# Attention units regrouped: both heads of a pair over 128 queries, scores as three 64-row products per head

## The chip, the cores and the metric

The kernel runs on one core of a Trainium2 chip. The metric is the device time of one execution in microseconds (us); the median of the runs is compared. Durations of single instructions come from one profiled execution.

## What is computed

One decoder layer on x of 1024 positions by 1024 features, float32. After an RMS norm one projection feeds two attention branches of eight heads each (head width 64): branch A is causal attention over the 256 keys that an indexer selects for each query, branch B is a causal dilated attention whose three patterns are merged. Both have an RMS norm on each head's queries and keys and a bias by relative position. Gates, an output projection and the residual follow.

```python
def reference(x, norm_gain, w_in, w_out, rel_bias, q_norm_a, k_norm_a, q_norm_b, k_norm_b):
    ...
        xn = rms_norm(x, norm_gain[layer])
        proj = jnp.einsum('bsd,de->bse', xn, w_in[layer])
        qa, ka, va, za, qi, ki, wi, qb, kb, vb, zb = jnp.split(proj, split_points, axis=-1)
        qa = rms_norm(qa.reshape(b, s, N_HEADS_A, HEAD_DIM), q_norm_a[layer])
        ka = rms_norm(ka.reshape(b, s, N_HEADS_A, HEAD_DIM), k_norm_a[layer])
        ...
        a_out = dsa_attention(qa, ka, va, qi, ki, wi, bias_a)
        b_out = dilated_attention(qb, kb, vb, bias_b)
        mixed = jnp.concatenate([a_out.reshape(b, s, D_A) * jax.nn.silu(za),
                                 b_out.reshape(b, s, D_B) * jax.nn.silu(zb)], axis=-1)
        x = x + jnp.einsum('bse,ed->bsd', mixed, w_out[layer])
    return x
```

In both branches a head's core is softmax(q k^T / 8 + bias + mask) v; the kernel computes it densely over all causal keys, with the selection or the dilation in the bias.

## The kernel before

Every float32 operand of a large product is split into a high part of type fp32r and a remainder ("hi" and "lo"), and a product is taken as two or three products of such parts. The work is done in eight pairs of heads (`make_pair`, L422), each pair's q, k, v and gate columns projected together. For each pair and each of eight blocks of 128 positions, `proj_item` (L434) issues 24 products of 512 columns (L445 to L447), scales and normalises the result, and keeps v as a hi and a lo part (L464 to L466). Its `finish2` (L480) splits k into `k`, where a head's 64 hi columns stand beside its 64 lo columns; `later` (L494) transposes that on TensorE, so that the tile `kst` holds, for each head, 64 rows of hi over 64 rows of lo.

Attention works on units (`make_unit`, L550). A unit is one head of a pair over two query blocks, 2s and 2s+1, that is 256 queries; a pair has four values of s and two heads, eight units in all, 64 in the program.

- `split_q` (L527) writes q as hi, lo, hi in 192 columns per block and head; `transpose_q` (L535) makes of it two stationary operands of 128 rows, hi over lo and lo over hi. For each of the two query blocks it issues four transposes into a PSUM tile (pool tag "tr", one buffer) and ScalarE casts it to `qt` (L544).
- `scores` (L555) takes a query block against up to 512 keys (a chunk): two products of 128 rows (L566, L567), both into one PSUM tile `sp` (tag "s", two buffers). VectorE adds the bias and keeps a running minimum (L573); in branch A, GpSimd first adds the selection mask to the bias (L571). When the last chunk is done, ScalarE takes the exponential and its sum (L583). The results stand in tiles `L` (six buffers, shared with scratch of the key selection).
- `pt` (L594) transposes the exponentials of two key blocks and both query blocks into one PSUM tile of up to 512 columns (L600), and splits it into `pth` (ScalarE, L604) and `ptl` (VectorE, L605).
- `pv` (L608) multiplies by v: for each key block a product of 256 columns (both query blocks) with `pth` and one with `ptl` (L618); the last key block of a unit has 128 columns (L616). The stationary operand is v of one key block and head, 128 columns: hi and lo beside each other.
- `make_gate` and `combine` (L629, L637) add the halves, divide, gate and store.

`run_slot` (L789) sets the order in which all this is written: in slot k stand the scores of unit k+1, the transposes and value products of unit k, the combine of the unit before, a share of the projection of a later pair (`place`, L781, by the table `gw`), and in the first half of the program steps of the key selection on VectorE (L266). The framework's scheduler then orders the instructions of each engine. TensorE takes its queue in order.

Of the kernel before, what the change touches and what calls it, by code (L numbers as in the profile page):

```python
# [10 lines left out]
F32 = mybir.dt.float32  # L11
# [35 lines left out]
def kernel(ctx: ExitStack, tc: tile.TileContext, xT, x, w_idx, w_pair, w_out, gain,  # L47
# [10 lines left out]
    def f32(ap):  # L58
        return ap.bitcast(F32)
# [99 lines left out]
    def dup_hi(t, h):  # L159

        return t.rearrange("p h (a d) -> p h a d", d=HD)[:, :h, 0:3:2, :]
# [272 lines left out]
    def proj_item(p, tb):  # L434
# [45 lines left out]
        def finish2():  # L480
            if j == 1:
                return
            raw, mu = duo["raw"], duo["mu"]
            kk = raw[:, :, 2:4, :]
            p.eng.tensor_tensor(kk, kk, mu[:, :, 2:4].unsqueeze(3).to_broadcast([P, 2, 2, HD]), OP.mult)
            k = rg.tile([P, 2, 2, P], F32R, name="k", tag="ktok", bufs=CFG["kb"])
            nc.scalar.copy(k[:, :, :, 0:64], kk)
            p.eng.tensor_tensor(k[:, :, :, 64:128], kk, f32(k[:, :, :, 0:64]), OP.subtract)
            duo["k"] = k
            q = rg.tile([P, 2, 2, HD], F32, name="q", tag="q", bufs=CFG["q"])  # L490
            p.eng.tensor_tensor(q, raw[:, :, 0:2, :], mu[:, :, 0:2].unsqueeze(3).to_broadcast([P, 2, 2, HD]), OP.mult)
            p.q[tb // 2] = q

        def later():  # L494
            if j == 1:
                return
            pk = ps.tile([P, 2, 2, P], F32R, name="pk", tag="tr", bufs=CFG["tr"])
            for b in range(2):
                for h in range(2):
                    nc.tensor.transpose(pk[:, h, b, :], duo["k"][:, b, h, :], identr)  # L500
# [3 lines left out]
            nc.scalar.copy(p.k[s][:, :, o:o + 2 * P], f32(pk.rearrange("p h b t -> p h (b t)")))  # L504

        it.groups = [lambda kt=kt: group(kt) for kt in range(KT)]
        def weight(kt):
# [18 lines left out]

    def split_q(p, s):  # L527

        q = p.q[s].rearrange("p b h d -> p (b h) d")
        hl = sb.tile([P, 4, 192], F32R, name="qhl", tag="qhl", bufs=CFG["qhl"])  # L530
        nc.scalar.copy(dup_hi(hl, 4), q.unsqueeze(2).to_broadcast([P, 4, 2, HD]))
        p.eng.tensor_tensor(hl[:, :, 64:128], q, f32(hl[:, :, 0:64]), OP.subtract)
        p.hl[2 * s] = p.hl[2 * s + 1] = hl

    def transpose_q(p, s):  # L535
        hl = p.hl[2 * s]
        for qb in (2 * s + 1, 2 * s):
            pq = ps.tile([P, 512], F32R, name="pq", tag="tr", bufs=CFG["tr"])
            for h in range(2):
# [3 lines left out]
            qt = sb.tile([P, 2, 2, P], F32R, name="qt", tag="qT", bufs=CFG["qT"])  # L543
            nc.scalar.copy(qt.rearrange("p a b c -> p (a b c)"), f32(pq))  # L544
            p.hl[qb] = qt

    class Block:
        pass

    def make_unit(p, s, h, blk):  # L550
        u = Unit()
        u.p, u.s, u.h, u.blk = p, s, h, blk
        L, mns = {}, {}

        def scores(qb, ci, last):  # L555
            nk = (qb + 1) * P
            col0 = S - P - P * qb
            c0 = 512 * ci
            w = min(512, nk - c0)
            if qb not in mns:  # L560
                mns[qb] = [sm.tile([P, 2], F32, name="mn", tag="mn"), 0]
            mn, done = mns[qb]
# [5 lines left out]
            l = sb.tile([P, 512], F32, name="L", tag="L", bufs=CFG["L"])  # L568
            bias = p.T[h][:, col0 + c0:col0 + c0 + w]
            if p.is_a and qb >= 2:  # L570
                nc.gpsimd.tensor_tensor(l[:, :w], bias, sc[qb][:, c0:c0 + w], OP.add)  # L571
                bias = l[:, :w]
            nc.vector.tensor_tensor_reduce(l[:, :w], sp[:, :w], bias, -1.0,  # L573
                                           3e38 if done == 0 else mn[:, done - 1:done],
                                           OP.add, OP.min, mn[:, done:done + 1])
            mns[qb][1] = done + 1
            L[qb, ci] = l
            if last:
                j = qb - 2 * s
                for c in range(len(chunks_of(qb))):  # L580
                    w = min(512, nk - 512 * c)
                    l = L[qb, c][:, :w]
                    nc.scalar.activation(l, l, AF.Exp, bias=mn[:, done:done + 1], scale=-1.0,  # L583
                                         accum_out=blk.den[:, j, h, c:c + 1])

        u.S = []
        for qb in (2 * s + 1, 2 * s):
            cs = list(range(len(chunks_of(qb))))[::-1]
            for c in cs:
                u.S.append(lambda qb=qb, c=c, last=(c == cs[-1]): scores(qb, c, last))  # L590

        T = {}

        def pt(kp):  # L594
            t = ps.tile([P, 512], F32, name="pt", tag="ptp", bufs=CFG["ptp"])
            slots = [(2 * kp, 2 * s), (2 * kp, 2 * s + 1)]
            slots += [(2 * kp + 1, 2 * s), (2 * kp + 1, 2 * s + 1)] if kp < s else [(2 * kp + 1, 2 * s + 1)]
            for si, (kb, qb) in enumerate(slots):
                o = (kb % 4) * P
                mark(nc.tensor.transpose(t[:, si * P:(si + 1) * P], L[qb, kb // 4][:, o:o + P], identf))  # L600
            w = len(slots) * P
# [4 lines left out]
            T[kp] = th, tl  # L606

        def pv(kp):  # L608
            if kp == 0 and h == 0:
                blk.po = ps.tile([P, 2, 256], F32, name="po", tag="o", bufs=CFG["o"])  # L610
            po = blk.po
            for j in range(2):
                vv = p.v[kp][:, j, 2 * h:2 * h + 2, :].rearrange("p a b -> p (a b)")
                for n, t in enumerate(T[kp]):
                    if j and kp == s:
                        nc.tensor.matmul(po[:, h, 128:256], vv, t[:, 256:384], start=False, stop=(n == 1))  # L616
                    else:
# [4 lines left out]
        for kp in range(s + 1):  # L622
            u.B.append(lambda kp=kp: pt(kp))
            if kp:
                u.B.append(lambda kp=kp: pv(kp - 1))
        u.B.append(lambda: pv(s))
        return u

    def make_gate(p, s, blk):  # L629
# [90 lines left out]
    for p in pairs:  # L720
        for s in range(3, -1, -1):
            blk = Block()
            blk.p, blk.s = p, s
            for h in range(2):
                units.append(make_unit(p, s, h, blk))

    def unit(k):
        return units[k] if 0 <= k < len(units) else None
# [60 lines left out]
    def run_slot(k):  # L789
# [7 lines left out]
            ev.append(((t - g0) / (g1 - g0), f))  # L797
        att = []
        u = unit(k - 1)
        if u and u.h == 1:  # L800
            att.append(lambda: combine(u.p, u.s, u.blk))
        w = unit(k + 2)
        if w and w.h == 0:
            for h in range(2):
                if h not in w.p.T:
                    ev.append((0.0, lambda h=h: w.p.T.__setitem__(h, load_T(2 * w.p.n + h))))
            ev.append((CFG["sq"], lambda: split_q(w.p, w.s)))
            ev.append((CFG["qt"], lambda: transpose_q(w.p, w.s)))
        a = []
        un = unit(k + 1)  # L810
        if un:
            if un.h == 0:
# [4 lines left out]
        if v and v.h == 1:  # L817
# [82 lines left out]
```

## Time and profile before

| | |
|---|---|
| time, median of 3 runs (lowest to highest) | 821.43 us (818.26 to 826.37) |
| the profiled execution: its own time, and its span | 824.92 us, 823.2 us |
| TensorE (PE) busy, of the span | 774.1 us, 94% |
| TensorE weight loads (PEld) | 658.5 us, 80% |
| VectorE (DVE) | 590.5 us, 72% |
| ScalarE (ACT) | 492.5 us, 60% |
| GpSimd (POOL) | 435.0 us, 53% |
| mean granted clock of TensorE, share of full | 0.975 |

Each TensorE product has a weight load (PEld) and a matmul (PE). Matmuls are pipelined: a record of 0.39 us overlaps the next one's, so the price of a product in a stream is the distance from its start to the next start, not its own duration. A form such as "128*128 128x512" reads: 128 rows by 128 columns of stationary operand, 512 columns streamed, 128 rows of result.

### The profile page before, as it was taken

What the parts mean: (1) busy time and instruction counts of PE and PEld (TensorE: products, weight loads), DVE (VectorE), ACT (ScalarE), POOL (GpSimd) and SP (SyncE); (2) the same over time, 40 slices, a digit from 0 to 9 for tenths busy, and PEclk for the clock granted to TensorE, in tenths of its full rate; (3) what the DMA queues carried; (4) which work ended last, traced back from release to release, by engine and by line L of the source; (5) the groups of instructions that cost most, each with busy time, mean ns of one, the idle gap of its engine ahead of it and who ended that gap; (6) DMA issues with size and microseconds to landing.
All of it is one profiled execution on the core that took longest, in us unless ns stands there. A gap on an engine that the chain in (4) does not pass through costs nothing.

```text
span 823.2 us, 12893 instructions
## 1 busy us (share of the span) xinstructions
PE 774.1 (94%) x4302; PEld 658.5 (80%) x4302; DVE 590.5 (72%) x1366; ACT 492.5 (60%) x1156; POOL 435.0 (53%) x453
## 2 busy tenths in 40 slices
PE   5999989999999999999999699999998998999996
PEld 4778857888888888878887588878887886788874
DVE  6834778878999989997578777567755775667621
ACT  6834466567676766767675376757774675456400
POOL 6942536347533833574278867755555575435320
PEclk9999998999999999999999799999998999999999
DMA  8679005003200510141013100410162225725775
GB/s 296 234 226 297 4 2 189 15 14 103 77 14 14 141 52 1 33 123 53 2 52 103 39 14 14 120 61 14 27 166 77 65 75 184 241 95 193 219 219 183
DMA packets 52053, 83.34 MB, mean 101 GB/s; under 512 B 5632, under 2 KB 23312, under 8 KB 51984
## 3 DMA queue, kind: packets, MB, share of 16 engines
q1 hardware_dynamic: 47376, 74.10, 29.2%
q0 software_dynamic: 4608, 8.39, 3.8%
q8 instruction: 34, 0.56, 0.3%
q14 instruction: 35, 0.29, 0.1%
HBM read 65.62 MB, written 26.29 MB: 112 GB/s over the span
## 4 chain that ended last, share of the span: by engine, by line
PE 35%; DVE 8%; DMA 5%; ACT 2%; issue 1%; POOL 1%; SPq 0%; DVEq 0%; POOLq 0%; ACTq 0%
PE pp L445 4%; PE pp L446 4%; PE pp L447 4%; PE po L618 4%; PE pt L600 4%; PE pp L672 3%; PE pp L674 3%; PE pp L673 3%; PE sp L566 2%; PE sp L567 2%; DVE jk L245 1%; DMA mo<-mixl_d 1%; DVE ptl L605 1%; DMA raw<-in_w_pair_dram 1%; DMA raw<-in_w_out_dram 1%
## 5 line engine op out<-in xcount | busy, mean ns | idle before, releaser
L445 PE MATMUL pp<-wh,xh 128*128 128x512 f32 x512 | 210.7, 414 | 1.0 <-ACT wh L84 1.0
L446 PE MATMUL pp<-wl,xh 128*128 128x512 f32 x512 | 203.2, 397 | 1.4 <-POOL wl L85 1.4
L447 PE MATMUL pp<-wh,xl 128*128 128x512 f32 x512 | 202.9, 397 | 0.0
L583 ACT ACTIVATE L<-L,mn 128x512 f32<-128x512 f32 (+1 forms) x192 | 117.4, 613 | 60.0 <-DVE mn L573 59.2
L571 POOL TENSOR_TENSOR L<-T,sc 128x512 f32<-128x512 f32 (+3 forms) x80 | 90.2, 1150 | 62.1 <-PE pt L600 46.9
L605 DVE TENSOR_TENSOR ptl<-pt,pth 128x512 fp32r<-128x512 f32 (+1 forms) x160 | 100.2, 632 | 30.9 <-ACT pth L604 29.7
L85 POOL TENSOR_TENSOR wl<-raw,wh 128x512 fp32r<-128x512 f32 x68 | 90.9, 1346 | 57.5 <-ACT wh L84 53.1
L604 ACT CAST pth<-pt 128x512 fp32r<-128x512 f32 (+1 forms) x160 | 85.6, 542 | 47.8 <-PE pt L600 45.1
L447 PEld LDWEIGHTS pp<-wh,xl 128*128 128x128 f32 x512 | 97.3, 190 | 19.8
L446 PEld LDWEIGHTS pp<-wl,xh 128*128 128x128 f32 x512 | 98.0, 191 | 17.7 <-POOL wl L85 2.3
L445 PEld LDWEIGHTS pp<-wh,xh 128*128 128x128 f32 x512 | 97.8, 191 | 17.6 <-ACT wh L84 2.2
L600 PE MATMUL pt<-identr,L 128*128 128x128 f32 x576 | 88.1, 275 | 0.8 <-ACT L L583 0.8
L266 DVE TENSOR_SCALAR_CACHE_REDUCE waste<-sc,thr 128x640 int8<-128x640 f32 (+5 forms) x90 | 84.6, 940 | 0.8
L618 PE MATMUL po<-ptl,v 128*128 128x256 f32 x256 | 71.2, 295 | 11.2 <-DVE ptl L605 11.2
L618 PE MATMUL po<-pth,v 128*128 128x256 f32 x256 | 72.8, 295 | 1.6 <-DVE mx L646 1.4
L566 PE MATMUL sp<-kst,qt 128*128 128x512 f32 (+1 forms) x192 | 71.6, 375 | 0.0
L600 PEld LDWEIGHTS pt<-identr,L 128*128 128x128 f32 x576 | 66.2, 141 | 4.7 <-ACT L L583 1.2
L567 PE MATMUL sp<-kst,qt 128*128 128x512 f32 (+1 forms) x192 | 68.2, 355 | 0.0
L84 ACT CAST wh<-raw 128x512 fp32r<-128x512 f32 x80 | 48.5, 618 | 32.7 <-DMA raw<-in_w_pair_dram 24.3
L618 PEld LDWEIGHTS po<-ptl,v 128*128 128x128 f32 x256 | 48.8, 191 | 18.1 <-DVE ptl L605 14.2
L462 POOL TENSOR_TENSOR mu<-ss,mhalf 128x8 f32<-128x8 f32 x32 | 54.4, 1699 | 12.4 <-DVE ss L460 11.5
L453 ACT ACTIVATE praw<-pp,rr 128x512 f32<-128x512 f32 x64 | 43.7, 685 | 28.2 <-PE pp L447 27.8
(150 smaller groups left out, 1677.8 us busy)
## 6 DMA issues: line engine op xcount, KB each, us to landing
raw<-in_w_pair_dram SPq DMA_DIRECT2D x64, 256.0 KB, 2.8
skew<-rowd SPq DMA_DIRECT2D x16, 576.0 KB, 13.9
T<-skew SPq DMA_DIRECT2D x16, 512.0 KB, 3.6
stage<-in_x_dram SPq DMA_DIRECT2D x16, 256.0 KB, 5.4
mixh_d<-mh SPq DMA_DIRECT2D x32, 128.0 KB, 2.2
mixl_d<-ml SPq DMA_DIRECT2D x32, 128.0 KB, 2.1
raw<-in_w_out_dram SPq DMA_DIRECT2D x16, 256.0 KB, 3.3
mo<-mixh_d POOLq DMA_DIRECT2D x16, 256.0 KB, 3.6
```

The costliest lines, as they stand in the source:

```text
L85: (eng or nc.gpsimd).tensor_tensor(lo, raw, f32(hi), OP.subtract)
L445: pace(nc.tensor.matmul(pp, xh[tb][:, kt, :], hi, start=(kt == 0), stop=False))
L446: nc.tensor.matmul(pp, xh[tb][:, kt, :], lo, start=False, stop=False)
L447: nc.tensor.matmul(pp, xl[tb][:, kt, :], hi, start=False, stop=(kt == KT - 1))
L566: mark(nc.tensor.matmul(sp[:, :w], qt[:, h, 0, :], kk, start=True, stop=False))
L567: nc.tensor.matmul(sp[:, :w], qt[:, h, 1, :], kk, start=False, stop=True)
L571: nc.gpsimd.tensor_tensor(l[:, :w], bias, sc[qb][:, c0:c0 + w], OP.add)
L583: nc.scalar.activation(l, l, AF.Exp, bias=mn[:, done:done + 1], scale=-1.0, accum_out=blk.den[:, j, h, c:c + 1])
L600: mark(nc.tensor.transpose(t[:, si * P:(si + 1) * P], L[qb, kb // 4][:, o:o + P], identf))
L604: nc.scalar.copy(th[:, :w], t[:, :w])
L605: nc.vector.tensor_tensor(tl[:, :w], t[:, :w], f32(th[:, :w]), OP.subtract)
L618: nc.tensor.matmul(po[:, h, :], vv, t[:, 256 * j:256 * j + 256], start=(kp == 0 and j == 0 and n == 0), stop=False)
```

## The change

A unit is now one query block of 128 queries for both heads of a pair (still eight units a pair). `k` and `q` are split with the two heads beside each other: one half of the tile holds the hi part of both heads, the other the lo part, so that after the transposes head 0 stands on partitions 0 to 63 and head 1 on 64 to 127. `split_q` no longer writes hi twice, and `transpose_q` issues four transposes and one cast for both query blocks together. A score is three products of 64 rows for each head (hi by hi, hi by lo, lo by hi), written with the heads in turns, each head into its own `sp`. `pt` takes one head and one chunk; `pv` multiplies 128 columns at a time, key block by key block, first all of `pth`, then all of `ptl`. The pool sizes and the table `gw` stay.

```diff
@@ finish2
-            nc.scalar.copy(k[:, :, :, 0:64], kk)
-            p.eng.tensor_tensor(k[:, :, :, 64:128], kk, f32(k[:, :, :, 0:64]), OP.subtract)
+            kk = kk.rearrange("p b h d -> p b (h d)")
+            nc.scalar.copy(k[:, :, 0, :], kk)
+            p.eng.tensor_tensor(k[:, :, 1, :], kk, f32(k[:, :, 0, :]), OP.subtract)
...
@@ split_q, transpose_q
-        nc.scalar.copy(dup_hi(hl, 4), q.unsqueeze(2).to_broadcast([P, 4, 2, HD]))
-        p.eng.tensor_tensor(hl[:, :, 64:128], q, f32(hl[:, :, 0:64]), OP.subtract)
+        nc.scalar.copy(hl[:, :, 0, :], q)
+        p.eng.tensor_tensor(hl[:, :, 1, :], q, f32(hl[:, :, 0, :]), OP.subtract)
...
-        for qb in (2 * s + 1, 2 * s):
-            pq = ps.tile([P, 512], F32R, name="pq", tag="tr", bufs=CFG["tr"])
-            for h in range(2):
-                t = hl[:, 2 * (qb % 2) + h, :]
-                nc.tensor.transpose(pq[:, (2 * h) * P:(2 * h + 1) * P], t[:, 0:128], identr)
-                nc.tensor.transpose(pq[:, (2 * h + 1) * P:(2 * h + 2) * P], t[:, 64:192], identr)
...
+        pq = ps.tile([P, 512], F32R, name="pq", tag="tr", bufs=CFG["tr"])
+        for j in (1, 0):
+            for a in range(2):
+                nc.tensor.transpose(pq[:, (2 * j + a) * P:(2 * j + a + 1) * P], hl[:, j, a, :], identr)
...
@@ scores
-            sp = ps.tile([P, 512], F32, name="sp", tag="s", bufs=CFG["s"])
-            qt = p.hl[qb]
-            kk = p.k[ci][:, h, :w]
-            mark(nc.tensor.matmul(sp[:, :w], qt[:, h, 0, :], kk, start=True, stop=False))
-            nc.tensor.matmul(sp[:, :w], qt[:, h, 1, :], kk, start=False, stop=True)
+            qt, kk = p.hl[u.s], p.k[ci]
+            sp = [ps.tile([P, 512], F32, name="sp", tag="s", bufs=CFG["s"]) for h in range(2)]
+            for n, (a, b) in enumerate(((0, 0), (0, 1), (1, 0))):
+                for h in range(2):
+                    r = slice(HD * h, HD * h + HD)
+                    m = nc.tensor.matmul(sp[h][:, :w], qt[r, j, a, :], kk[r, b, :w], start=(n == 0), stop=(n == 2))
...
@@ pt, pv
-                        nc.tensor.matmul(po[:, h, :], vv, t[:, 256 * j:256 * j + 256],
-                                         start=(kp == 0 and j == 0 and n == 0), stop=False)
...
+            po = blk.po[:, h, P * j:P * j + P]
+            w = min(512, nk - c)
+            for n, t in enumerate(T[h, c]):
+                for o in range(0, w, P):
+                    kb = (c + o) // P
+                    vv = p.v[kb // 2][:, kb % 2, 2 * h:2 * h + 2, :].rearrange("p a b -> p (a b)")
+                    nc.tensor.matmul(po, vv, t[:, o:o + P], start=(c == chunks[0] and n == 0 and o == 0),
+                                     stop=(c == chunks[-1] and n == 1 and o == w - P))
```

How the instructions stand in TensorE's queue is shown at two places. The first is the score products of the first pair where its attention begins; `sp` is the PSUM tile of a score, `kst` the transposed keys, `qt` the transposed queries, `pp` a projection's PSUM tile. Before, a chunk has two products into one tile:

```order
L566 MATMUL sp_1491<-kst_1106,qt_1477 128x512
L567 MATMUL sp_1491<-kst_1106,qt_1477 128x512
L566 MATMUL sp_1507<-kst_1385,qt_1477 128x512
L567 MATMUL sp_1507<-kst_1385,qt_1477 128x512
L445 MATMUL pp_1403<-wh_1305,xh7_464 128x512
L445 MATMUL pp_1460<-wh_1305,xh6_425 128x512
L566 MATMUL sp_1541<-kst_1106,qt_1484 128x384
L567 MATMUL sp_1541<-kst_1106,qt_1484 128x384
```

Now the queue's first scores are these (a "x3" marks three equal rows in a row):

```order
L569 MATMUL sp_1486<-kst_1106,qt_1477 128x512
L569 MATMUL sp_1487<-kst_1106,qt_1477 128x512
L569 MATMUL sp_1486<-kst_1106,qt_1477 128x512
L569 MATMUL sp_1487<-kst_1106,qt_1477 128x512
L569 MATMUL sp_1486<-kst_1106,qt_1477 128x512
L569 MATMUL sp_1487<-kst_1106,qt_1477 128x512
L542 MATMUL pq_1693<-identr_84,qhl_1623 128x128 x4
L445 MATMUL pp_1403<-wh_1305,xh7_464 128x512
L445 MATMUL pp_1460<-wh_1305,xh6_425 128x512
L569 MATMUL sp_1537<-kst_1385,qt_1477 128x512 x3
L446 MATMUL pp_1403<-wl_1306,xh7_464 128x512
L447 MATMUL pp_1403<-wh_1305,xl7_465 128x512
```

The first chunk stands with the heads in turns, as the code writes it; of the second chunk, the three products of head 0 (`sp_1537`) stand together, and those of head 1 follow ten rows of projection later. Over the whole program the 576 score products stand in 165 runs between other work: 27 of them are six products strictly in turns, 60 are three products of a single head, 14 are three of one head followed by three of the other.

The second place is the first value products (`po`) of the same pair, on TensorE too; `pt` is a PSUM tile of transposed exponentials, `v` the values. Before:

```order
L618 MATMUL po_1606<-pth_1579,v_1395 128x256
L618 MATMUL po_1606<-ptl_1580,v_1395 128x256
L600 MATMUL pt_1626<-identr_84,L_1544 128x128
L600 MATMUL pt_1626<-identr_84,L_1494 128x128
L600 MATMUL pt_1626<-identr_84,L_1544 128x128
L600 MATMUL pt_1626<-identr_84,L_1494 128x128
L618 MATMUL po_1606<-pth_1597,v_1264 128x256
L618 MATMUL po_1606<-ptl_1598,v_1264 128x256
L618 MATMUL po_1606<-pth_1597,v_1264 128x256
L618 MATMUL po_1606<-ptl_1598,v_1264 128x256
```

Now:

```order
L615 MATMUL po_1611<-ptl_1577,v_1116 128x128 x2
L615 MATMUL po_1611<-ptl_1577,v_830 128x128 x2
L599 MATMUL pt_1628<-identr_84,L_1498 128x128 x4
L615 MATMUL po_1611<-pth_1588,v_1395 128x128 x2
L615 MATMUL po_1611<-pth_1588,v_1264 128x128 x2
L615 MATMUL po_1611<-ptl_1589,v_1395 128x128 x2
L615 MATMUL po_1611<-ptl_1589,v_1264 128x128 x2
L599 MATMUL pt_1651<-identr_84,L_1547 128x128 x4
```

A value product of 256 columns has become two of 128, each with a weight load of its own; the transposes between them are as many as before. TensorE's queue holds 1152 value products of 128 columns, where it held 512 of 256 and 128 of 128.

## Rows read from the trace of the kernel before

**Rows 1.** By stretch: us; PE, PEld, DVE, ACT, POOL busy; clock; DMA; GB/s

```profile
200.00:300.00 100.00, 98.30 (x581) 84.84 (x580) 90.48 (x253) 68.89 (x165) 55.16 (x65) 1.00 0.24 69
...
sum 823.00, PE 774.08 PEld 658.50 DVE 590.53 ACT 492.51 POOL 434.97; mean PE 77.41 PEld 65.85 DVE 59.05 ACT 49.25 POOL 43.50
```

**Rows 2.** Waits of TensorE: waiter, releaser, us in total, times, longest us

```profile
PE po L618 <- DVE ptl L605: 11.2, 10, 2.3
PE pq L541 <- ACT qt L544: 8.4, 10, 3.6
...
PE pi L176 <- ACT wih L104: 0.3, 1, 0.3
```

**Rows 3.** Groups of TensorE by form: count, busy us, mean ns, idle us before

```profile
L618 PE MATMUL po<-pth,v 128*128 128x256 f32 x256 | 72.8, 295 | 1.6 <-DVE mx L646 1.4
...
L541 PE MATMUL pq<-identr,qhl 128*128 128x128 f32 x128 | 26.6, 254 | 12.2 <-ACT qt L544 8.4 <-POOL qhl L532 2.1 <-ACT kst L504 1.8
...
L616 PE MATMUL po<-pth,v 128*128 128x128 f32 x64 | 14.4, 224 | 0.0
```

**Rows 4.** The score products of line 566: count, durations ns min/median/max, first and last start, forms

```profile
L566 PE MATMUL sp<-kst,qt x192: 220/389/755, 126.4 to 776.9; 128*128 128x512 f32 x96, 128*128 128x384 f32 x32, 128*128 128x256 f32 x32, 128*128 128x128 f32 x32
```

**Rows 5.** TensorE in order of time: start us, duration us, instruction (transposes, value products, scores)

```profile
308.40 0.34 PE L567 MATMUL sp<-kst,qt 128*128 128x384 f32 x1
308.58 0.23 PE L541 MATMUL pq<-identr,qhl 128*128 128x128 f32 x1
...
308.87 0.35 PE L618 MATMUL po<-pth,v 128*128 128x256 f32 x1
309.06 0.39 PE L566 MATMUL sp<-kst,qt 128*128 128x512 f32 x1
309.29 0.39 PE L567 MATMUL sp<-kst,qt 128*128 128x512 f32 x1
309.51 0.28 PE L618 MATMUL po<-ptl,v 128*128 128x256 f32 x1
309.63 0.28 PE L618 MATMUL po<-pth,v 128*128 128x256 f32 x1
```

**Rows 6.** TensorE in order of time: eight transposes of 128 columns, then two projection products

```profile
305.96 1.03 PE L600 MATMUL pt<-identr,L 128*128 128x128 f32 x8
306.75 0.47 PE L445 MATMUL pp<-wh,xh 128*128 128x512 f32 x1
307.07 0.40 PE L446 MATMUL pp<-wl,xh 128*128 128x512 f32 x1
```

**Rows 7.** TensorE in order of time: two score products of 128 columns, then two of 512

```profile
316.69 0.22 PE L566 MATMUL sp<-kst,qt 128*128 128x128 f32 x1
316.75 0.28 PE L567 MATMUL sp<-kst,qt 128*128 128x128 f32 x1
316.86 0.45 PE L445 MATMUL pp<-wh,xh 128*128 128x512 f32 x1
317.14 0.40 PE L446 MATMUL pp<-wl,xh 128*128 128x512 f32 x1
```

**Rows 8.** TensorE in order of time: a stationary operand of 32 rows after ones of 128

```profile
37.06 0.34 PE L217 MATMUL sp<-kist,qit 128*128 128x384 f32 x1
37.23 0.34 PE L218 MATMUL sp<-kist,qit 128*128 128x384 f32 x1
37.50 1.03 PE L393 MATMUL pb<-oh,rb 32*16 32x512 f32 x2
```

**Rows 9.** TensorE in order of time: a one-column stationary operand among full ones

```profile
395.15 0.39 PE L447 MATMUL pp<-wh,xl 128*128 128x512 f32 x1
395.47 0.19 PE L346 MATMUL pf<-bad,ranks 128*1 128x6 f32 x2
395.60 0.38 PE L618 MATMUL po<-ptl,v 128*128 128x256 f32 x1
395.82 0.28 PE L618 MATMUL po<-pth,v 128*128 128x256 f32 x1
```

**Rows 10.** Group of VectorE's bias-and-minimum step for 512 columns: count, busy us, mean ns

```profile
L573 DVE CUSTOM_DVE_ANT_0 L<-sp,T,mn 128x512 f32<-128x512 f32 x32 | 23.9, 746 | 3.9 <-PE sp L567 2.8
```

More of the change, by code (lines that the diff above doesn't have):

```diff
@@ L527, in split_q @@
     def split_q(p, s):
[L529 to L545 removed]
+        q = p.q[s].rearrange("p b h d -> p b (h d)")
@@ new lines, in split_q @@
+        hl = sb.tile([P, 2, 2, P], F32R, name="qhl", tag="qhl", bufs=CFG["qhl"])
+        nc.scalar.copy(hl[:, :, 0, :], q)
+        p.eng.tensor_tensor(hl[:, :, 1, :], q, f32(hl[:, :, 0, :]), OP.subtract)
+        p.hl[s] = hl
+    def transpose_q(p, s):
+        hl = p.hl[s]
+        pq = ps.tile([P, 512], F32R, name="pq", tag="tr", bufs=CFG["tr"])
+        for j in (1, 0):
+            for a in range(2):
+                nc.tensor.transpose(pq[:, (2 * j + a) * P:(2 * j + a + 1) * P], hl[:, j, a, :], identr)
+        qt = sb.tile([P, 2, 2, P], F32R, name="qt", tag="qT", bufs=CFG["qT"])
+        nc.scalar.copy(qt.rearrange("p a b c -> p (a b c)"), f32(pq))
+        p.hl[s] = qt
@@ L547, with make_unit, scores @@
     class Block:
         pass
-    def make_unit(p, s, h, blk):
+    def make_unit(p, qb, blk):
         u = Unit()
[L552 to L556, printed above, removed]
+        u.p, u.qb, u.s, u.blk = p, qb, qb // 2, blk
+        j = qb % 2
+        nk = (qb + 1) * P
+        chunks = chunks_of(qb)[::-1]
+        L = {}
+        mns = {}
+        def scores(c0):
+            ci = c0 // 512
             col0 = S - P - P * qb
-            c0 = 512 * ci
@@ L569, in scores @@
[L569 to L590, printed above, removed]
+            qt, kk = p.hl[u.s], p.k[ci]
@@ new lines, in scores @@
+            sp = [ps.tile([P, 512], F32, name="sp", tag="s", bufs=CFG["s"]) for h in range(2)]
[3 more added lines that the diff above has]
+                    m = nc.tensor.matmul(sp[h][:, :w], qt[r, j, a, :], kk[r, b, :w], start=(n == 0), stop=(n == 2))
+                    if n == 0 and h == 0:
+                        mark(m)
+            for h in range(2):
+                if c0 == chunks[0]:
+                    mns[h] = sm.tile([P, 2], F32, name="mn", tag="mn")
+                mn, done = mns[h], chunks.index(c0)
+                l = sb.tile([P, 512], F32, name="L", tag="L", bufs=CFG["L"])
+                bias = p.T[h][:, col0 + c0:col0 + c0 + w]
+                if p.is_a and qb >= 2:
+                    nc.gpsimd.tensor_tensor(l[:, :w], bias, sc[qb][:, c0:c0 + w], OP.add)
+                    bias = l[:, :w]
+                nc.vector.tensor_tensor_reduce(l[:, :w], sp[h][:, :w], bias, -1.0,
+                                               3e38 if done == 0 else mn[:, done - 1:done],
+                                               OP.add, OP.min, mn[:, done:done + 1])
+                L[h, ci] = l
@@ L592, in make_unit, with pt @@
+            if c0 == chunks[-1]:
+                for h in range(2):
+                    for n, c in enumerate(chunks):
+                        l = L[h, c // 512][:, :min(512, nk - c)]
+                        nc.scalar.activation(l, l, AF.Exp, bias=mns[h][:, len(chunks) - 1:len(chunks)], scale=-1.0,
+                                             accum_out=blk.den[:, j, h, n:n + 1])
+        u.S = [lambda c=c: scores(c) for c in chunks]
         T = {}
-        def pt(kp):
+        def pt(h, c):
@@ L595, in pt @@
             t = ps.tile([P, 512], F32, name="pt", tag="ptp", bufs=CFG["ptp"])
[L596 to L601, printed above, removed]
+            w = min(512, nk - c)
@@ L605, in pt, with pv @@
             nc.vector.tensor_tensor(tl[:, :w], t[:, :w], f32(th[:, :w]), OP.subtract)
-            T[kp] = th, tl
-        def pv(kp):
-            if kp == 0 and h == 0:
+            T[h, c] = th, tl
+        def pv(h, c):
+            if j == 1 and (h, c) == order[0]:
                 blk.po = ps.tile([P, 2, 256], F32, name="po", tag="o", bufs=CFG["o"])
[L611 to L617, printed above, removed]
-                        nc.tensor.matmul(po[:, h, :], vv, t[:, 256 * j:256 * j + 256],
-                                         start=(kp == 0 and j == 0 and n == 0), stop=False)
-        u.B = []
[L622 to L626, printed above, removed]
+            po = blk.po[:, h, P * j:P * j + P]
+            w = min(512, nk - c)
+            for n, t in enumerate(T[h, c]):
+                for o in range(0, w, P):
+                    kb = (c + o) // P
+                    vv = p.v[kb // 2][:, kb % 2, 2 * h:2 * h + 2, :].rearrange("p a b -> p (a b)")
+                    nc.tensor.matmul(po, vv, t[:, o:o + P], start=(c == chunks[0] and n == 0 and o == 0),
+                                     stop=(c == chunks[-1] and n == 1 and o == w - P))
+        order = [(h, c) for h in range(2) for c in chunks]
+        u.B = []
+        for n, hc in enumerate(order):
+            u.B.append(lambda hc=hc: pt(*hc))
+            if n:
+                u.B.append(lambda hc=order[n - 1]: pv(*hc))
+        u.B.append(lambda: pv(*order[-1]))
         return u
@@ L723 @@
             blk.p, blk.s = p, s
-            for h in range(2):
-                units.append(make_unit(p, s, h, blk))
+            for qb in (2 * s + 1, 2 * s):
+                units.append(make_unit(p, qb, blk))
     def unit(k):
@@ L799, in run_slot @@
         u = unit(k - 1)
-        if u and u.h == 1:
+        if u and u.qb % 2 == 0:
             att.append(lambda: combine(u.p, u.s, u.blk))
         w = unit(k + 2)
-        if w and w.h == 0:
+        if w and w.qb % 2:
             for h in range(2):
@@ L816, in run_slot @@
         b = list(v.B) if v else []
-        if v and v.h == 1:
+        if v and v.qb % 2 == 0:
             b.insert(int(len(b) * CFG["gpos"]), lambda: make_gate(v.p, v.s, v.blk))
```

11 lines of the change are left out of this document (4 added, 7 removed).

## The prediction

> **What bounds the kernel now.** I read the busy times by stretch first. In 200 to 300 us, in the middle of attention, TensorE is busy for 98.3 of 100 us, VectorE for 90.5, ScalarE for 68.9, GpSimd for 55.2; over the whole span VectorE has 590.5 of 823 [rows 1]. A busy TensorE need not be at its peak, so next comes the list of its waits: the longest entry is 11.2 us (value products for `ptl`), then 8.4 us (query transposes for the cast of the transposes before), and all 18 entries, down to one of 0.3, add up to 45 us of 823 [rows 2]. What is left is a stream in which one product starts when the one before lets it, so the kernel is bound by the sum of the start-to-start distances on TensorE. The timeline gives these prices. A product of 512 columns costs 0.23 us (309.06 to 309.29 to 309.51), of 384 columns about 0.17 (308.40 to 308.58 is 0.18; 37.06 to 37.23 is 0.17), of 256 columns 0.12 (309.51 to 309.63) [rows 5, 8]. A product of 128 columns is not half of that. Eight transposes start at 305.96, the next product at 306.75, and that one takes 0.32 instead of 0.23 until its follower at 307.07: 1.11 less 0.23 over eight is 0.11 each [rows 6]. Two ordinary products of 128 columns start at 316.69 and 316.75, and the product behind them lets its own follower start only at 317.14: 0.45 less 0.23 over two is again 0.11 [rows 7]. So below 256 columns it is the weight load that counts, and it takes 0.11 however narrow the product is. The fp32r transposes of the queries are a little cheaper: four from 308.58 to 308.87, with 0.07 more on the 256-column product behind them (0.19 against 0.12), make 0.09 each [rows 5].
>
> **The change, part by part.**
>
> *Value products.* Before: 512 of 256 columns (256 with `pth`, as many with `ptl`) and 128 of 128 columns (64 and 64) [rows 3], 512 x 0.12 + 128 x 0.11 = 75.5 us. After: 1152 of 128 columns, by the queue. They stream the same number of columns, but each has its own load: 1152 x 0.11 = 126.7 us. That is +51 us. Bounds: if each cost only the 0.06 that the first of a pair shows (316.69 to 316.75), 69 us and -6; if each cost as much as a 256-column product, 138 us and +63. I take 0.11, the value of the run of eight and of the pair [rows 6, 7], because the queue has them in runs of two to eight.
>
> *Query transposes.* 256 become 128 (line 541 has 128 of them [rows 3], line 542 as many): -128 x 0.09 = -11.5 us. The wait of the second four for the cast of the first (8.4 us [rows 2]) has no place any more, since there is one group and one cast: -8.4. Together -20 us, between -11 and -22.
>
> *Score products.* Before: two lines of 96, 32, 32 and 32 products of 512, 384, 256 and 128 columns [rows 4]: 2 x (96 x 0.23 + 32 x 0.17 + 32 x 0.12 + 32 x 0.11) = 69.8 us. After, three for two: 104.6 us if one follows the other, +35. What comes off is the overlap of two heads on the two halves of the rows. No row of before shows such a pair. From the queue, 136 pairs of neighbours from different heads can be formed (59, 13, 31 and 33 of the four widths), not 288, because the heads stand in turns in only 27 of the 165 runs. If each such pair costs one product, 59 x 0.23 + 13 x 0.17 + 31 x 0.12 + 33 x 0.11 = 23 us come off, and the part is +12. If the two weight loads of a pair still follow each other at 0.11, a pair costs at least 0.22, and only 16 us come off (59 x 0.23, 13 x 0.12, 31 x 0.02): +19. I take +19, because the loads follow each other in every row that I have; the ends are +12 and +35.
>
> *Entering and leaving the 64-row form.* All big products before use the array whole. Three products of another size stand among them, and the trace shows what that costs. Behind the 384-column product at 37.23 the 32-row product starts only at 37.50: 0.27 against 0.17 [rows 8]. Behind the 512-column product at 395.15 the one-column product starts at 395.47: 0.32 against 0.23. On the way back the first 256-column product takes until its follower 0.22 instead of 0.12, since its load and the next were not taken early [rows 9]. So a change of form costs 0.09 to 0.10 for the stop, and up to 0.10 more for a load that can't be hidden. The queue has 165 runs of scores, thus 330 changes of form: 30 us for the stops alone, 66 with the loads. The narrow products have their load in the price of 0.11 already, so I take the middle, 0.15 each: +50 us. The lower end is 0, if 64 rows and 128 rows count as the same form, the upper 66. The Trainium skill says in "TensorEngine Tiling (Array Packing)", section "Key Properties", that changing the tiling mode, and not merely the tile, drains TensorE; the stops in rows 8 and 9 agree with it, though none is a change between 64 and 128 rows. By that rule every run pays twice; without it this part is 0. The skill's "TensorE: Matmul & The Clock Gate", Part 3, holds out the opposite gain, that products on different row groups start about 4 ns apart; by it the score part would be the +12 above, and no row here shows it.
>
> *The other engines.* ScalarE loses 32 casts of `qt` and half of the query split, and gets 32 more casts of `pth` at the same columns; VectorE gets 32 more subtractions at the same columns; GpSimd is unchanged. With ScalarE at 69 and VectorE at 90 of 100 us in that stretch [rows 1], and TensorE's work growing there, their additions lie beside it: 0. The scores of a chunk now take both `sp` buffers at once, so a chunk waits for two VectorE steps, each 0.75 us at 512 columns [rows 10]; behind the waiting product stands TensorE's whole queue. No entry of the list of waits is for a score today, with the same two buffers, and the queue puts other products between the chunks: 0, as a rival below otherwise. A longer TensorE gives `ptl` more time, so I take half of its 11.2 us off: -6.
>
> *Sum.* 51 - 20 + 19 + 50 - 6 = +94 us on the profiled execution's 824.9 us: 919. That execution stood 3.5 us above the median of the runs, so I forecast 821.4 + 94 = 915 us.
>
> **The rivals.**
>
> *No stop between 64 and 128 rows.* Everything else as above, without the 50 us: 865 us. For it: rows 8 and 9 show other sizes (32 rows, one column), not this one. Against: all three stops have the same size, whatever the form.
>
> *No overlap of the heads.* The 64-row products run one after the other: +16 us, 931 us. For it: nothing in the trace shows two products at once. Against: the two halves hold different operands and write different PSUM tiles, and what they share on the trace's showing, the loads, is counted already.
>
> *The score buffers become the wait.* If each of the 96 chunks waited half a VectorE step, 96 x 0.37 = 36 us, it would be 951 us. Against: no score waits today.
>
> *The loads hide, and the kernel is not slower.* If TensorE took weight loads early enough, a 128-column value product would cost 0.06, as the first of a pair does in rows 7, and changes of form would cost nothing for the same reason: -6 - 20 + 12 - 6 = -20, 801 us. It decides in the value products: below 0.08 us each (75 + 20 - 12 + 6 = 89 us over 1152) the change gains. Against: the run of eight keeps 0.11 to its end, and the second of the pair pays what the first saved.
>
> **How the numbers follow.** I give the forecast 0.55, no stop 0.22, no overlap 0.12, the score buffers 0.06, hidden loads 0.05. The first four are all slower by 5 to 16%; the last is 2.5% faster, and mixtures of it end near no change. A difference of 1% is about what a measurement of this kernel can tell from none. Faster by over 1%: 0.04, within 1%: 0.03, slower: 0.93. The range reaches down to the case without stops with a little off its value products, 858, and up past the case of the score buffers, 955; only hidden loads and sums of several bad cases lie outside.
>
> **What would show it.** In the trace of the changed kernel: value products of line 615 starting 0.11 us apart in their runs (0.06 would give the last rival); in front of a first score product of line 569, and in front of the product behind the last one, a distance larger by 0.09 to 0.2 than the columns explain (none would give the first rival); neighbours of different heads starting well under 0.2 us apart at 512 columns, and of the same head 0.23 apart (0.23 for both would give the second); no large wait of line 569 for the bias-and-minimum step; no wait of the query transposes for `qt`. TensorE's busy share should stay at its level over a longer span, and VectorE's and ScalarE's shares fall. The prediction is wrong if the time is under 858, above all if value products cost 0.06 or TensorE shows new waits for other engines that make up most of the difference.

## The result and the profile after

The changed kernel takes 900.33 us (median of 3 runs, 898.68 to 902.35) against 821.43 us before: the ratio is 1.095, with a 95% interval of 1.086 to 1.105. The forecast was 915 us, in a range of 858 to 955.

The profile page of the changed kernel begins (busy us, share of the span, instructions):

```profile
span 896.9 us, 14109 instructions
...
PE 863.9 (96%) x4878; PEld 695.2 (78%) x4878; DVE 586.8 (65%) x1398; ACT 472.9 (53%) x1156; POOL 435.2 (49%) x453
```

TensorE's share rose from 94 to 96% over a longer span, and everything else fell in share: the added time is on TensorE. Its waits, in the same view as [rows 2]:

```profile
PE po L615 <- DVE ptl L603: 7.2, 2, 6.4
...
PE sp L569 <- ACT qt L544: 1.9, 6, 0.7
PE sp L569 <- DVE mn L581: 1.7, 1, 1.7
...
PE pq L542 <- ACT qhl L532: 1.0, 1, 1.0
```

The wait of the query transposes for `qt` (8.4 us) is gone, the one for `ptl` went from 11.2 to 7.2, and scores wait 1.7 us in all for the bias-and-minimum step. All entries together were 45 us and are 29. So the kernel waits less and is slower. The groups by form, as in [rows 3, 4]:

```profile
L615 PE MATMUL po<-ptl,v 128*128 128x128 f32 x576 | 95.1, 274 | 7.3 <-DVE ptl L603 7.2
L615 PE MATMUL po<-pth,v 128*128 128x128 f32 x576 | 92.9, 269 | 2.0 <-DVE mx L644 1.1 <-ACT pth L602 0.8
L569 PE MATMUL sp<-kst,qt 64*128 64x512 f32 x288 | 77.4, 442 | 3.6 <-ACT qt L544 1.9 <-DVE mn L581 1.7
...
L542 PE MATMUL pq<-identr,qhl 128*128 128x128 f32 x128 | 16.9, 253 | 2.0 <-ACT qhl L532 1.0 <-POOL qhl L533 1.0
```

The counts are those of the prediction. What they cost is read from the timeline of TensorE (start us, duration us, instruction). Three value products among products of 512 columns:

```profile
303.18 0.40 PE L445 MATMUL pp<-wh,xh 128*128 128x512 f32 x1
303.42 0.45 PE L615 MATMUL po<-pth,v 128*128 128x128 f32 x3
303.70 0.44 PE L446 MATMUL pp<-wl,xh 128*128 128x512 f32 x1
303.99 0.40 PE L447 MATMUL pp<-wh,xl 128*128 128x512 f32 x1
```

From 303.42 to 303.99 is 0.57; less 0.23 for the product of 512 columns, 0.34 for three, 0.11 each, as forecast. Next, a chunk whose six score products stand in turns, between a group of transposes and a projection:

```profile
166.34 0.62 PE L599 MATMUL pt<-identr,L 128*128 128x128 f32 x4
166.90 0.96 PE L569 MATMUL sp<-kst,qt 64*128 64x512 f32 x6
167.79 0.50 PE L446 MATMUL pp<-wl,xh 128*128 128x512 f32 x1
168.13 0.39 PE L447 MATMUL pp<-wh,xl 128*128 128x512 f32 x1
```

and one with three products of a single head, between projections:

```profile
233.52 0.39 PE L447 MATMUL pp<-wh,xl 128*128 128x512 f32 x1
233.84 0.96 PE L569 MATMUL sp<-kst,qt 64*128 64x512 f32 x3
234.74 0.50 PE L445 MATMUL pp<-wh,xh 128*128 128x512 f32 x1
235.07 0.40 PE L446 MATMUL pp<-wl,xh 128*128 128x512 f32 x1
```

Six products in turns take 0.89 us, three of one head 0.90. So the two heads do run side by side; in the records a product of the second head starts 0 to 16 ns behind that of the first, 4 in the median. But three times 0.23 is 0.68, and both runs take 0.21 more. In front of the second run, 233.52 to 233.84 is 0.32 instead of 0.23, and the projection behind it takes 0.33 instead of 0.23 to its follower. I put all this down to the change between 128 and 64 rows; the run with full rows below tests it. The weight loads around the first run show where the time goes:

```profile
166.37 0.36 PEld L599 LDWEIGHTS pt<-identr,L 128*128 128x128 f32 x3
166.90 0.53 PEld L569 LDWEIGHTS sp<-kst,qt 64*128 64x128 f32 x6 [0.17 <-issue]
167.79 0.19 PEld L446 LDWEIGHTS pp<-wl,xh 128*128 128x128 f32 x1 [0.36 <-issue]
167.90 0.19 PEld L447 LDWEIGHTS pp<-wh,xl 128*128 128x128 f32 x1
```

The load of the first score starts at 166.90 with its product, and that of the projection at 167.79 with its own; in a stream of one form a load starts while the product before still runs. In these rows the idle time in front is put down to "issue", that is to nothing that the profile shows.

I summed the start-to-start distances of all TensorE records by kind of product:

| us | before | after | difference |
|---|---|---|---|
| value products | 91.8 | 137.9 | +46.1 |
| scores | 78.0 | 109.8 | +31.8 |
| query transposes | 27.0 | 13.6 | -13.4 |
| transposes of exponentials | 55.4 | 63.3 | +7.9 |
| projections | 371.1 | 381.7 | +10.6 |
| all others (output, indexer, k, gates) | 189.9 | 181.3 | -8.6 |

A distance belongs to the product that begins it, so the stop ahead of a run stands with its neighbours, the transposes and projections, and a wait stands with the product before it: of the value products' distances 10.2 us were idle time before and 8.5 are after.

### The profile page after: what moved, and what is told of

Same layout as the page of the kernel before. It is cut to its first block, busy times and chain, and to the rows that moved or that the text cites. A ratio compares the mean times of both kernels' runs of the same rounds, so it can differ in the third digit from the quotient of the medians.

```text
span 896.9 us, 14109 instructions
## 1 busy us (share of the span) xinstructions
PE 863.9 (96%) x4878; PEld 695.2 (78%) x4878; DVE 586.8 (65%) x1398; ACT 472.9 (53%) x1156; POOL 435.2 (49%) x453
## 4 chain that ended last, share of the span: by engine, by line
PE 77%; DMA 7%; DVE 6%; POOL 4%; issue 4%; ACT 2%; SPq 1%; POOLq 0%; ACTq 0%; DVEq 0%
PE po L615 12%; PE pp L445 12%; PE sp L569 11%; PE pp L446 11%; PE pp L447 11%; PE pt L599 7%; PE pp L670 3%; PE pp L672 3%; PE pp L671 3%; DMA stage<-in_x_dram 3%; POOL wl L85 2%; DMA raw<-in_w_pair_dram 1%; PE pk L501 1%; PE pq L542 1%; PE pg L639 1%
## 5 line engine op out<-in xcount | busy, mean ns | idle before, releaser
L589 ACT ACTIVATE L<-L,mn 128x512 f32<-128x512 f32 (+3 forms) x192 | 116.9, 611 | 50.8 <-DVE mn L581 50.3
L603 DVE TENSOR_TENSOR ptl<-pt,pth 128x512 fp32r<-128x512 f32 (+3 forms) x192 | 104.9, 553 | 56.8 <-ACT pth L602 55.5
L602 ACT CAST pth<-pt 128x512 fp32r<-128x512 f32 (+3 forms) x192 | 89.7, 477 | 87.2 <-PE pt L599 85.1
L569 PE MATMUL sp<-kst,qt 64*128 64x512 f32 (+3 forms) x576 | 121.3, 386 | 3.6 <-ACT qt L544 1.9
L615 PE MATMUL po<-ptl,v 128*128 128x128 f32 x576 | 95.1, 274 | 7.3 <-DVE ptl L603 7.2
L615 PEld LDWEIGHTS po<-pth,v 128*128 128x128 f32 x576 | 87.0, 190 | 16.5 <-issue 2.3
L615 PEld LDWEIGHTS po<-ptl,v 128*128 128x128 f32 x576 | 83.3, 191 | 17.4 <-DVE ptl L603 8.4
L569 PEld LDWEIGHTS sp<-kst,qt 64*128 64x128 f32 x576 | 65.4, 187 | 38.8 <-issue 17.5
L615 PE MATMUL po<-pth,v 128*128 128x128 f32 x576 | 92.9, 269 | 2.0 <-DVE mx L644 1.1
L649 POOL TENSOR_TENSOR ml<-mx,mh 128x256 fp32r<-128x256 f32 x32 | 25.3, 792 | 89.8 <-ACT mh L648 85.9
```

The costliest lines, as they stand in the source:

```text
L569: m = nc.tensor.matmul(sp[h][:, :w], qt[r, j, a, :], kk[r, b, :w], start=(n == 0), stop=(n == 2))
L589: nc.scalar.activation(l, l, AF.Exp, bias=mns[h][:, len(chunks) - 1:len(chunks)], scale=-1.0, accum_out=blk.den[:, j, h, n:n + 1])
L615: nc.tensor.matmul(po, vv, t[:, o:o + P], start=(c == chunks[0] and n == 0 and o == 0), stop=(c == chunks[-1] and n == 1 and o == w - P))
```

## Experiments

Each ran beside the kernel before on the same chip; ratios are against that kernel, with 95% intervals.

**One part alone: value products of 128 columns.**

```diff
@@ pv of the kernel before
-                        nc.tensor.matmul(po[:, h, :], vv, t[:, 256 * j:256 * j + 256],
-                                         start=(kp == 0 and j == 0 and n == 0), stop=False)
+                        for c in range(2):
+                            nc.tensor.matmul(po[:, h, P * c:P * c + P], vv, t[:, 256 * j + P * c:256 * j + P * c + P],
+                                             start=(kp == 0 and j == 0 and n == 0 and c == 0), stop=False)
```

> The kernel before with one part of the change alone: each value product of 256 columns is issued as two of 128, with the same stationary operand. Nothing else changes. My theory (a product of 128 columns costs 0.11 us, because its weight load does): 512 more products, 512 x (2 x 0.11 - 0.12) = +51 us, 872 us, a little less if other waits shrink (860 to 875). The rival of hidden loads (0.06 each): no change, 815 to 825. The waits for ptl should not grow.

Measured: 863.12 us, ratio 1.049 (1.045 to 1.053), +40.5 us. The value products' distances are 131.8 us, against 1152 x 0.11 = 126.7 by price. The wait for `ptl` fell:

```profile
PE po L619 <- DVE ptl L605: 5.0, 7, 1.8
PE pq L541 <- ACT qt L544: 4.4, 7, 0.7
```

Those two waits were 11.2 and 8.4 [rows 2], so of the 51 us some ten were paid out of waits (all idle time in front of TensorE's products fell from 45 to 35 us). The same columns with the same operands, only cut in two, cost 5% of the kernel. Hidden loads are excluded.

**The heads held in turns by a critical section.**

```diff
@@ scores of the changed kernel
-            for n, (a, b) in enumerate(((0, 0), (0, 1), (1, 0))):
+            with tc.tile_critical():
+                for n, (a, b) in enumerate(((0, 0), (0, 1), (1, 0))):
...
-                    if n == 0 and h == 0:
-                        mark(m)
```

> The changed kernel with the six score products of a chunk held together by a critical section of the scheduler, so that all stand with the heads in turns; the pace mark on the first score product is left out. The queue then has 89 runs of scores instead of 165, and 288 pairs of neighbours of different heads instead of 136. My theory, with the distances of the changed kernel's trace (a whole change of form in and out costs 0.40 us a run, a pair costs one product): 76 x 0.40 = 30 us and 29 us of overlap come off, 900 - 59 = 841 us (835 to 855). If the change of form cost only its stop of 0.18 in and out: 900 - 14 - 29 = 857. The rival of the score buffers: a chunk must find both buffers free, TensorE waits for the bias-and-minimum step before scores, and the time stays at 885 or above.

Measured: 1016.46 us, ratio 1.238 (1.234 to 1.242). A miss, and not by the rival's mechanism either. The waits of TensorE:

```profile
PE sp L570 <- ACT L L588: 29.8, 10, 3.7
PE sp L570 <- issue: 27.8, 37, 5.9
PE sp L570 <- DVE mx L643: 14.2, 6, 2.5
PE sp L570 <- DMA raw<-in_w_pair_dram: 6.2, 1, 6.2
```

The scores wait for exponentials, for the combine, even for a weight transfer, of which a score needs none. These are some 120 us of new waits (idle time in front of products sums to 150 us in this trace, against 29). The critical section is the likely cause: its own line, L566, puts a DRAIN into TensorE's queue for each of the 96 chunks, and the changed kernel has none among its scores (count, ns min/median/max, first and last start):

```profile
L566 PEldq DRAIN  x96: 237/817/1505, 129.2 to 968.7; - x96
```

Whether the pace mark that was left out adds to the waits was not tested. The run says nothing of what the turns are worth. The experiment was made again without the section, below.

**No change of form: scores of 128 rows with zeros.**

```diff
@@ transpose_q and scores of the changed kernel (phase["qz"]: two tiles, zeroed once)
-                nc.tensor.transpose(pq[:, (2 * j + a) * P:(2 * j + a + 1) * P], hl[:, j, a, :], identr)
...
+                nc.tensor.transpose(pq[:, a * P:(a + 1) * P], hl[:, j, a, :], identr)
+            qt = phase["qz"][j]
+            for h in range(2):
+                nc.scalar.copy(qt[HD * h:HD * h + HD, h], f32(pq)[HD * h:HD * h + HD, :2 * P])
...
-                    m = nc.tensor.matmul(sp[h][:, :w], qt[r, j, a, :], kk[r, b, :w], start=(n == 0), stop=(n == 2))
+                    m = nc.tensor.matmul(sp[h][:, :w], qt[j][:, h, P * a:P * a + P], kk[:, b, :w], start=(n == 0), stop=(n == 2))
```

> The changed kernel with score products of 128 rows: the stationary operand of a head has zeros on the other head's 64 rows, so nothing changes form and no two products can run side by side. The transposes stand in two groups of two again, one for each query block, with two half casts each. My theory: no change of form, 165 x 0.40 = 66 us off, the overlap of 136 pairs lost, 23 us on, up to 8 us on for the wait of the second group: 857 to 870 us. If a change of form costs only its stop (30 us): 893 to 901. If it costs nothing: 920 or above. The distance before a first score product should be what the columns say.

Measured: 888.50 us, ratio 1.080 (1.078 to 1.082): 12 us under the changed kernel's 900, where 30 to 43 were expected; the time lies outside each of the three ranges. The mechanism is there; a chunk in its timeline:

```profile
163.88 0.39 PE L447 MATMUL pp<-wh,xl 128*128 128x512 f32 x1
164.11 1.55 PE L569 MATMUL sp<-kst,qz 128*128 128x512 f32 x6
165.50 0.39 PE L445 MATMUL pp<-wh,xh 128*128 128x512 f32 x1
165.72 0.39 PE L446 MATMUL pp<-wl,xh 128*128 128x512 f32 x1
```

0.23 in front, 1.39 for six products one after the other (6 x 0.23), 0.22 behind: no stop, no late load, and no overlap. The transposes of the exponentials fall from 63.3 to 53.0 us, since no stop follows them, and the value products from 137.9 to 129.6, of which about half is less waiting. But the idle time in front of TensorE's products rose from 29 to 40 us (9.2 us of it value products waiting for the combine, against 1.1 in the changed kernel), and the mean granted clock is 0.981 against 0.990, which is some 8 us (below). So about half of the expected gain was lost again to waits and clock. The run shows that leaving out the row halves together with their overlap is cheaper than having both, not by how much the stops alone cost.

**Half the query transposes alone.**

```diff
@@ transpose_q of the kernel before (q split as in the change)
+        pq = ps.tile([P, 2, 2, P], F32R, name="pq", tag="tr", bufs=CFG["tr"])
+        for j in (1, 0):
+            for a in range(2):
+                nc.tensor.transpose(pq[:, a, j, :], hl[:, j, a, :], identr)
+        qt = sb.tile([P, 2, 2, 2, P], F32R, name="qt", tag="qT", bufs=1)
+        for h in range(2):
+            src = f32(pq)[HD * h:HD * h + HD]
+            nc.scalar.copy(qt[0:HD, h], src)
+            for a in range(2):
+                nc.scalar.copy(qt[HD:P, h, a], src[:, 1 - a])
```

> The kernel before with half the query transposes alone: q is split as in the change (hi of both heads, lo of both heads), four transposes instead of eight for two query blocks, and ScalarE writes the two stationary operands of each head by six casts, four of them to the other half of the partitions, into one buffer instead of two. Scores and value products as before. My theory: 128 x 0.09 = 11.5 us off, and up to 8 us of waits for the cast: 802 to 812 us. The rival: the longer chain on ScalarE (six casts, about 2.6 us, behind the last score of the block before) makes TensorE wait before the scores, and the time is 821 or above.

Measured: 839.44 us, ratio 1.020 (1.018 to 1.021): the rival. The query transposes take 10 us less (22.5 to 12.8, idle time taken off), and TensorE waits more (59 us of idle time in front of its products against 45):

```profile
PE po L621 <- ACT pth L607: 8.8, 9, 2.8
PE sp L569 <- ACT qt L546: 8.5, 10, 1.0
```

Neither entry was in the list before. Whether the six casts or the single buffer is to blame was not taken apart by a run. The trace speaks for the casts: they take 77.9 us of ScalarE, where the casts of `qt` took 37.4 before, and of the idle time in front of them only 0.3 us is a wait for scores that still read the buffer. The change itself needs no such casts, since each head's products use its own half of the rows.

**The heads in turns, by order alone.**

```diff
@@ scores of the changed kernel
                     if n == 0 and h == 0:
                         mark(m)
+                        if "red" in phase:
+                            tc.add_manual_dep(m.ins, phase["red"].ins.name,
+                                              mybir.DependencyInfo(mybir.DependencyClass.Sync, mybir.DependencyReason.DATA),
+                                              reason="both")
+                    else:
+                        tc.add_manual_dep(m.ins, prev.ins.name,
+                                          mybir.DependencyInfo(mybir.DependencyClass.NoSync, mybir.DependencyReason.DATA),
+                                          reason="turns")
+                    prev = m
...
-                nc.vector.tensor_tensor_reduce(l[:, :w], sp[h][:, :w], bias, -1.0,
+                phase["red"] = nc.vector.tensor_tensor_reduce(l[:, :w], sp[h][:, :w], bias, -1.0,
```

> The changed kernel with the heads kept in turns by order alone: the first score product of a chunk also depends on the bias-and-minimum step of the chunk before's second head (so it starts when both buffers are free), and each further product of the chunk stands behind the one before it in TensorE's queue. No critical section. The queue then has 129 runs of scores instead of 165, and 273 pairs instead of 136. My theory (0.37 us for a change of form in and out, as summed over the changed kernel's trace; a pair costs one product): 36 x 0.37 = 13 us and about 24 us of overlap come off TensorE's sum, 900 - 37 = 863 us; as in the runs before, a part of it may come back as waits: 860 to 880. The rival of the score buffers, as in the run with the critical section: waits of scores for VectorE eat it, 890 or above.

Measured: 872.32 us, ratio 1.061 (1.057 to 1.065): 28 us under the changed kernel and within the expectation. The trace has the 129 runs and 273 pairs, and the score distances fall from 109.8 to 79.9 us. The cost of asking for both buffers at once:

```profile
PE sp L570 <- DVE mn L591: 3.8, 4, 3.1
```

So most of the lost overlap was the scheduler's splitting of the turns, and the score buffers are no bound. Even so the kernel is 49 us slower than before.

**One part alone: scores of 64 rows, one head.**

```diff
@@ scores of the kernel before (q and k laid out as in the change)
-            kk = p.k[ci][:, h, :w]
-            mark(nc.tensor.matmul(sp[:, :w], qt[:, h, 0, :], kk, start=True, stop=False))
-            nc.tensor.matmul(sp[:, :w], qt[:, h, 1, :], kk, start=False, stop=True)
+            kk, r = p.k[ci], slice(HD * h, HD * h + HD)
+            for n, (a, b) in enumerate(((0, 0), (0, 1), (1, 0))):
+                m = nc.tensor.matmul(sp[:, :w], qt[r, a, :], kk[r, b, :w], start=(n == 0), stop=(n == 2))
```

> The kernel before with the score part of the change alone: units of one head over 256 queries and value products of 256 columns stay, but q and k are laid out as in the change, with half the query transposes, and a score is three products of 64 rows of that one head, with nothing beside it. The queue has 193 runs of 64-row products and 2 pairs. My theory: scores +35, 193 x 0.37 = 71 us for changes of form, query transposes -11 and up to -8 of waits: 821 + 87 to 821 + 95, less what waits give back (about 10 to 15): 890 to 910 us. If a change of form cost only its stop, 35 us: 857 to 870. If it cost nothing: 836.

Measured: 896.63 us, ratio 1.090 (1.086 to 1.094), within the expectation. Its scores take 144.5 us of distances against 78.0 before; 576 products one after the other would be 105 by price. The two parts alone add 40.5 and 73.5 us (896.63 less 823.18 of the kernel before beside it; the halved query transposes are in the second), 114 together, and the whole change 79. The difference of 35 is about what the change has and the parts have not: the overlap, 25 us by the records, and 28 runs of scores fewer (165 against 193), at 0.37 us each 10 us. That it fits so closely is in part luck, since waits and clock fell by different amounts in the three runs; with both taken out the difference is 39. The regrouping of the units by itself, with scores of 128 rows as before, was not run.

## Why the prediction was right

*Value products: +51 by price.* Right: 0.11 each in the changed kernel's timeline, +46 in the distances, +40 in time when done alone, the rest out of waits.

*Query transposes: -20.* Right: 10.5 us less in the distances when idle time is taken off (13.4 with it), against 11.5 by price, and the wait of 8.4 us gone.

*Scores: +19.* The overlap was right, the limit that I set it was not, and so the size was off. I let the two loads of a pair follow each other at 0.11, "because the loads follow each other in every row that I have". They don't where the halves differ. Six products of 128 columns in turns (the first two rows, from the changed kernel) take as long as three of one head (the last two, from the 64-row scores of one head):

```profile
717.31 0.55 PE L569 MATMUL sp<-kst,qt 64*128 64x128 f32 x6
717.79 0.50 PE L445 MATMUL pp<-wh,xh 128*128 128x512 f32 x1
...
400.86 0.55 PE L567 MATMUL sp<-kst,qt 64*128 64x128 f32 x3
401.34 0.50 PE L447 MATMUL pp<-wh,xl 128*128 128x512 f32 x1
```

Both take 0.48 us, where six loads one after the other would take 0.66. In the changed kernel's records the second pair of a run of 256 columns starts 0.12 us before the third, that of a run of 128 columns 0.11: a pair costs one product, loads included. On the chip 142 pairs started within 0.02 us of each other; by price that is 25 us off, so the term was +10. The starts, 4 ns apart in the median, agree with the about 4 ns that the Trainium skill gives ("TensorE: Matmul & The Clock Gate", Part 3).

*Changes of form: +50.* Right, a little low. Over the 165 runs, what a run and its two neighbours take beyond their prices sums to about 60 us, some 0.37 a run: about 0.09 for the stop on the way in, 0.10 for the first load, 0.09 for the stop on the way out, and 0.06 to 0.11 for the load after. The stops read off sizes of 32 rows and of one column [rows 8, 9] hold between 64 and 128 rows too; the rule of the Trainium skill ("TensorEngine Tiling (Array Packing)", "Key Properties") agrees with this, and the trace gives it this price. The rival without stops fell by these rows, and by the 64-row scores alone (897 us, where no cost would give 836).

*Waits: -6.* Nearly right. With the 8.4 us counted under the transposes, -14 was forecast; the idle time in front of products fell by 16, from 45 to 29, though the wait for `ptl` gave only 4 of it.

*What the sum left out.* By price, 51 - 11 + 35 - 25 + 60 is +110; the profiled execution grew by 74. The waits took 16 of it. The clock took some 11: its mean grant rose from 0.975 to 0.990, so the time at the lower of its two levels (1.2 instead of 2.4 GHz) fell from 41 us (0.025 x 2 x 823) to 18, and half of that time is lost. Some nine remain; a part of it stands in the table, where the scores before took 78.0 us against the 69.8 of their prices, so that the old scores were priced too low. The closeness of 915 to 900 is therefore in part luck: the scores were nine too high, the changes of form ten too low, and the clock was not in the sum.

*The rivals.* No overlap fell by the run of six in 0.89 us. The score buffers fell: 1.7 us of waits, and 3.8 when both were asked for at once. Hidden loads fell by the value products alone.

*What the change was worth.* Six score products in turns cost three product prices and 0.37; the four products of 128 rows that they replace cost four. That pays only where a product costs over 0.37 us, and the widest here costs 0.23. So by these prices the row halves lose at this length of run, held together or not. With the heads held in turns little of the loss is theirs, though: of the 49 us of that run the value products alone account for 40.5, which leaves some nine for the row halves and the halved transposes together. This is a difference between runs and no run of its own. None of the runs points to a version that beats the kernel before.

## What to carry to other kernels

Price a product by the distance to the next start, with a floor at the weight load: here 0.11 us for 128 columns, so cutting a product of 256 columns in two doubles it almost. Count how often TensorE's queue enters and leaves a form of fewer rows, as the scheduler leaves it and not as the code is written, and weigh 0.37 us for each such run against the overlap inside it. Where TensorE is the bound, waits and clock can take back a part of what is taken from it or added to it: of the 30 to 43 us expected from leaving out the changes of form, 12 arrived.

## What the runs showed of the hardware that was not expected

Two products on different halves of the rows share even the price of their weight loads: a pair of 128 columns every 0.11 us, as much as a single one.

The mean granted clock goes roughly with the idle time of TensorE over these runs: 0.932 with 150 us of idle time in front of products (the critical section), 0.971 with 59 (half the transposes), 0.975 with 45 (before), 0.978 with 35 (value products alone), 0.986 with 33 (turns by order), 0.990 with 29 (after); 0.981 stands beside 40 (full rows) and beside 29 (scores of one head), so idle time alone does not set it. In the kernel before, a deep fall stands behind a stretch with idle time on TensorE (the columns are those of [rows 1]):

```profile
440.00:460.00 20.00, 16.12 (x88) 13.14 (x86) 18.25 (x28) 8.75 (x24) 15.08 (x13) 0.96 0.27 85
460.00:480.00 20.00, 17.62 (x83) 14.81 (x84) 14.32 (x27) 11.39 (x27) 14.36 (x14) 0.78 0.10 27
480.00:500.00 20.00, 20.00 (x126) 17.68 (x126) 16.25 (x35) 13.28 (x34) 12.85 (x14) 1.00 0.00 1
```

TensorE is busy for 16 of 20 us, then runs part of the next stretch at the lower level of 1.2 GHz (mean grant 0.78), and is back at 2.4 GHz when it is busy throughout. The changed kernel has such a place too:

```profile
500.00:520.00 20.00, 14.64 (x63) 10.27 (x63) 14.29 (x25) 7.90 (x19) 16.50 (x16) 0.83 0.05 14
```

Over the whole span, though, it spends 18 us at the lower level against 41 before. A slower kernel that waits less can thus lose less to the clock, which the forecast had not counted.
